# One decoder step on one core: the first six k tiles of the down projection as four pairs by seven products

## The chip, the cores and the metric

The kernel runs on one core of a Trainium2 chip. The metric is the device time of one launch in microseconds (us). TensorE (PE) multiplies into PSUM; VectorE (DVE), ScalarE (ACT) and GpSimd (POOL) do the rest; SyncE (SP) and POOL issue the transfers between DRAM and SBUF that this text speaks of. Each engine works through its own queue in order.

## The reference

One layer of a decoder, for 512 prompt tokens and 8 x 8 sample tokens, all in float32. The part that matters here is the feed-forward block behind the second norm:

```python
a, val = jnp.split(h2 @ w_up, 2, axis=-1)                # 1024 -> 2 x 2816
ac, new_ffn = _causal_conv(a, ffn_buf, ffn_conv_w)       # width 3, along the tokens
x = x + g2 * ((jax.nn.gelu(ac, approximate=False) * val) @ w_down)   # 2816 -> 1024
```

## The kernel before

Activations lie transposed: 128 features by 576 token columns (512 prompt, 64 sample) are one tile. w_up gives 22 "up tiles" m = 0 to 21; each has a gate and a value half, a convolution of three taps, a gelu and a product, t. The 22 tiles t are the k tiles of the down projection, which has 8 output tiles, m = 0 to 7.

Float32 accuracy comes from splitting each operand into a high and a low part (`split`: ACT writes the high part, DVE subtracts it for the low one) and from three passes of TensorE: high by high, high by low, low by high. A full product (`product`) of n k tiles is 6n matmuls: three passes by two column groups of 256 and 320.

Up tiles 4 to 21 and the down projection's last eight k tiles use `pair_product` instead: a two-by-two block product with seven products in place of eight (after Strassen and Winograd), each of 12 matmuls of 288 columns. It runs through seven parts into three PSUM banks X, Y and Z. Between parts it calls functions that the caller hands over as steps 0 to 7: step 0 before part 1, step n after part n. Part 5 writes bank Y, DVE reads it (`gate1`, rows pad), and part 7 writes Y again. X of an up tile is read by `times` one job later (rows cy).

The weights of a pair come from `pair_weights`: two raw blocks ra and rb of eight k tiles, and four sums of halves in place (sums1: s3 and rb; sums2: ra twice), each 128 x 512. Then A (ah, al), B (bh, bl), C (ch, cl) and D (dh, dl) are split: h is ACT's high part (whi, wh), l is DVE's low part (wlo, wl). Weights of job n + 1 are prepared beside job n by `beside_pair`, which says at which step; raw blocks of job n + 2 are loaded.

The order before: up tiles 0 to 3 as full products, up 4 to 7 as pairs, the down projection of k tiles 0 to 7 as eight full products, up 8 to 21 as pairs, the down projection of k tiles 8 to 13 as eight full products with other work beside them, and that of k tiles 14 to 21 as pairs. From the second norm on PE, ACT and DVE run in the order of the code (`pinned`); POOL's and SP's queues are ordered by a scheduler. Line 114 is the helper that issues for all engines in order, so instructions are told apart by tile names.

POOL does small things here: the copies of the convolution's state (sto, pad<-stF), the sample columns of `times` (cy<-p,y), and DMAs that add while they transfer.

Of the kernel before, what the change touches and what calls it, by code (L numbers as in the profile page):

```python
# [16 lines left out]
P = 128  # L17
# [57 lines left out]
def step_kernel(ctx: ExitStack, tc: tile.TileContext, ins: dict, outs: list):  # L75
# [15 lines left out]
    def nm(s):  # L91
        cnt[0] += 1
        return f"{s}{cnt[0]}"
# [31 lines left out]
    def pf(ps):  # L125
        return ps[:, 256:832]
# [303 lines left out]
            self.low(self.x1, self.r1)  # L430
            self.low(self.n4, self.r0[:, :HT])

    def pair_weights(ra, rb, moved="", narrow=True):

        c0, c1 = slice(0, 4), slice(4, 8)
        w = {}

        def add(out, x, y):
            dve.tensor_tensor(out=out, in0=x, in1=y, op=ALU.add)

        def tiles():
            return [wp.tile([P, NK, P], F32R, tag=t, name=nm(t), bufs=S_BUFS) for t in ("whi", "wlo")]
# [12 lines left out]

        def s3_slots():
            if not narrow:
                return [x[:, 0:4, :] for x in tiles()]
            return slot("wh", F32R, [P, 4, P]), slot("wl", F32R, [P, 4, P])

        def sums1():
            w["raw"] = slot("s3", shape=[P, 4, P])
            add(w["raw"], ra[:, c0], rb[:, c0])
            add(rb[:, c0], rb[:, c0], rb[:, c1])

        def sums2():
            add(ra[:, c0], ra[:, c0], rb[:, c0])
            add(ra[:, c1], ra[:, c1], ra[:, c0])

        def named(n0, n1, name):  # L470
            hi, lo = w[name]
            w[n0] = (lambda k: hi[:, k, :]), (lambda k: lo[:, k, :])
            if n1:
                w[n1] = (lambda k: hi[:, k + 4, :]), (lambda k: lo[:, k + 4, :])
# [15 lines left out]
    def pair_product(w, x, steps, out_a0, out_a1, out_b0, out_b1, apart=False):  # L490

        X, Y = (halves(mmps())[1][:, :HT] if apart or n else aux()[:, :HT] for n in range(2))
        Z = aux()[:, :HT]
        p5 = slot("p5")[:, :HT]

        def part(bank, wn, xn_, more=True):

            (hi, lo), xs = w[wn], x[xn_]  # L500
            for k in range(4):
                xh, xl = xs[k]
                passes = (hi(k), xh), (hi(k), xl), (lo(k), xh)
                for n, (wt, xx) in enumerate(passes):
                    matmul(
                        bank, wt, xx, start=not more and k + n == 0, stop=k + n == 5,
                        skip_group_check=more,
                    )
# [1322 lines left out]
    class FfnTile:  # L1831
# [37 lines left out]
            self.t = conv_times(ps, self.y)  # L1869

        def high(self):
            if self.m >= FB:
                fc.append(self.t)
                return
            self.hi = slot("fh", F32R)
            act.activation(self.hi, self.t, AF.Copy)

        def low(self):
            if self.m >= FB:
                return  # L1880
            lo = slot("fl", F32R)
            dve.tensor_tensor(out=lo, in0=self.t, in1=self.hi.bitcast(F32), op=ALU.subtract)
            fa.append((self.hi, lo))

    class FfnPair(FfnTile):
# [6 lines left out]
        def prepare(self):  # L1892
            self.w, self.steps = pair_weights(*self.raws)
            return self.steps

        def run(self, steps):
# [22 lines left out]
        def times(self):  # L1919
# [5 lines left out]
                out=b8(sv(t)), in0=b8(self.x1[:, n:]), in1=b10(self.y)[:, :, 0:8], op=ALU.mult  # L1925
            )

    def merged(*parts):

        out = {}  # L1930
# [6 lines left out]
    def beside_pair(p, t):  # L1937
# [14 lines left out]

    def down_load(m, m0, m1):
# [27 lines left out]
    for dst, w in zip(first, ws):  # L1981
        for g, k in pend[-2:]:
            kstep(dst, w, h2, k, (g,))
    made2, made3, fa, fc = {}, {}, [], []

    tiles = [FfnTile(m) for m in range(4)]
    ops = [PairOperands(h2, kp, made2, h2_raw) for kp in range(4)]
# [71 lines left out]
    steps["dl"]()  # L2059

    n3 = [op.n3 for op in ops]
    pairs = {4: pair, 5: nxt}
    for m0, m1 in FCH:
        if m0:
            fa = []
        before = None
        for m in range(max(m0, 4), m1):
            pair = pairs.pop(m)
            beside = []
            if m == 4:  # L2070
                beside = [{
                    1: n3, 2: [tiles[3].gelu], 5: [lambda: tiles[3].times(v3)],
                    6: [tiles[3].high, tiles[3].low],
                }]
            if m + 1 < m1:
                if m + 2 < m1:
                    pairs[m + 2] = FfnPair(m + 2)
                beside.append(beside_pair(before, pairs[m + 1].prepare()))
            else:
                wd = {}  # L2080
                raw = [down_load(j, m0, min(m1, FB)) for j in range(4 if m1 > FB else 2)]
                beside.append(beside_pair(before, None))
                beside.append({2: [lambda: wd.update({0: split_w(raw[0])})],
                               5: [lambda: wd.update({1: split_w(raw[1])})]})
            pair.run(merged(*beside))
            before = pair
        if m1 == NF:
            break
        before.first_tap()
        before.taps()  # L2090
        before.gelu()
        before.times()
        before.high()
        before.low()
        if m1 < NF:
            pairs = {m1: FfnPair(m1)}
            steps = None
            ps = [mmps() for _ in range(2)]
            n = m1 - m0
            for k0, k1 in ((0, n - 2), (n - 2, n)):  # L2100
                for j in range(2):
                    for k in range(k0, k1):
                        kstep(halves(ps[j]), wd[j], fa, k)
            wd[2] = split_w(down_load(2, m0, m1))
            for j in range(2):
                residual(pf(ps[j]), x1[j], 40 + j)
            for m in range(2, NK):
                if m + 1 < NK:
                    wd[m + 1] = split_w(down_load(m + 1, m0, m1))
                acc_m = product(wd[m], fa)  # L2110
                if m == 4:
                    steps = in_turn(pairs[m1].prepare())
                    steps[0]()
                elif m > 4:
                    steps[m - 3]()
                if m == NK - 1:
                    pairs[m1 + 1] = FfnPair(m1 + 1)
                residual(acc_m, x1[m], 40 + m)
    acc3 = slot("acc")
    r3 = cp.tile([P, 8], F32, tag="r3", name="r3")  # L2120

# [37 lines left out]
        ops[kp].sums()  # L2159

    def next_down():
        wd[len(wd)] = split_w_moved(wd_raw.pop(len(wd)))

    def next_raw():
        j = len(wd) + len(wd_raw)
        wd_raw[j] = down_load(j, m0, FB)

    def finish():
        before.times()
# [117 lines left out]
```

## Time and profile before

| | us |
|---|---|
| median of three runs | 960.41 (959.83 to 961.05) |
| span of the profiled execution | 958.8 |
| busy: PE / DVE / ACT / POOL in the span | 944.6 / 725.8 / 549.1 / 132.9 |
| up tiles 4 to 7 as pairs end, old down stage begins | 653.4 |
| the old down stage ends, up tile 8 begins | 706.0 |
| the last down products begin, about | 857 |

The profile gives the span of its execution, from the first to the last instruction, and no separate launch time; the three runs lie 1.0 to 2.2 us above the span. Rows of the order of time read: start, length, engine, line, operation, out<-in, shape, count, and in brackets idle time before it and who ended it.

### The profile page before, as it was taken

The numbers are of one execution on the slowest core, as the hardware profiler recorded it, in microseconds if no ns is written. First come the engines' busy times: TensorE is split into PE (matmuls) and PEld (weight loads), VectorE is DVE, ScalarE is ACT, GpSimd is POOL, SyncE is SP. The second block draws the span as 40 slices with busy tenths as digits, with TensorE's granted clock in tenths as the row PEclk, the third lists the DMA queues.
The fourth block names the chain that finished last, engine by engine and source line by source line (L and its number), as shares of the span: only waits on it lengthen the run. The fifth ranks groups of instructions, "written<-read, shape, count | busy, mean of one in ns | idle before, by whom it ended". The sixth has DMA issues, their size and how long they took to land.

```text
span 958.8 us, 18738 instructions
## 1 busy us (share of the span) xinstructions
PE 944.6 (99%) x7290; PEld 909.4 (95%) x7290; DVE 725.8 (76%) x1355; ACT 549.1 (57%) x1058; POOL 132.9 (14%) x317
## 2 busy tenths in 40 slices
PE   7999999999999999999999999999999999999997
PEld 5799999999999899999889999999999999999997
DVE  4788988875876867876677588995559998968864
ACT  5474768745665447865344566653226565546664
POOL 2123121101201012210001130100000011101110
PEclk9999999999999999999999999999999999999999
DMA  9984233426546768799985732232323233228542
GB/s 275 332 249 110 77 93 100 150 71 172 122 128 201 237 220 215 198 247 285 302 282 113 185 86 66 85 106 67 110 89 90 88 90 109 84 82 173 128 96 99
DMA packets 182651, 144.09 MB, mean 150 GB/s; under 512 B 7688, under 2 KB 162124, under 8 KB 182274
## 3 DMA queue, kind: packets, MB, share of 16 engines
q1 hardware_dynamic: 172546, 111.72, 38.9%
q0 software_dynamic: 9872, 30.92, 14.1%
q8 instruction: 57, 0.93, 0.4%
q14 instruction: 32, 0.26, 0.1%
q10 hardware_dynamic: 144, 0.26, 0.1%
HBM read 113.89 MB, written 12.07 MB: 131 GB/s over the span
## 4 chain that ended last, share of the span: by engine, by line
PE 90%; DMA 3%; ACT 2%; issue 2%; DVE 1%; SPq 1%; POOL 0%; POOLq 0%; ACTq 0%; DVEq 0%
PE mm L114 50%; PE aux L114 37%; PE aux L1281 2%; PE aux L1185 2%; DMA ad<-in_w_ada 1%; SPq L538 1%; DMA wlo<-raw 1%; DMA raw<-in_w_down 1%; ACT whi L114 1%; DMA x<-in_x_prompt 1%; ACT wlo L114 0%; ACT xh L114 0%; ACT sg L114 0%; ACT nh L114 0%; DVE tl L114 0%
## 5 line engine op out<-in xcount | busy, mean ns | idle before, releaser
L114 ACT ACTIVATE whi<-raw 128x1024 fp32r<-128x1024 f32 (+3 forms) x186 | 188.8, 1023 | 81.7 <-DVE raw L114 28.4
L114 DVE TENSOR_TENSOR wlo<-raw,whi 128x1024 fp32r<-128x1024 f32 (+2 forms) x163 | 192.3, 1185 | 37.0 <-ACT whi L114 36.2
L114 PE MATMUL aux<-2l,whi 128*128 128x288 f32 (+2 forms) x232 | 68.4, 295 | 0.0
L114 PE MATMUL aux<-2h,whi 128*128 128x288 f32 (+2 forms) x232 | 68.3, 295 | 0.0
L114 PE MATMUL aux<-2h,wlo 128*128 128x288 f32 (+2 forms) x232 | 68.3, 295 | 0.0
L114 DVE TENSOR_TENSOR raw<-raw 128x512 f32<-128x512 f32 x88 | 61.6, 700 | 2.8
L114 PE MATMUL mm<-hh,whi 128*128 128x256 f32 (+2 forms) x264 | 60.6, 303 | 0.5 <-ACT hh L114 0.5
L114 PE MATMUL mm<-hh,wlo 128*128 128x256 f32 (+2 forms) x264 | 58.3, 295 | 0.0
L114 PE MATMUL aux<-hh,whi 128*128 128x288 f32 (+1 forms) x196 | 57.5, 300 | 0.0
L114 PE MATMUL mm<-hl,whi 128*128 128x256 f32 (+2 forms) x264 | 57.4, 295 | 0.1
L114 PE MATMUL aux<-hl,whi 128*128 128x288 f32 (+1 forms) x196 | 56.5, 295 | 0.0
L114 PE MATMUL aux<-hh,wlo 128*128 128x288 f32 (+1 forms) x196 | 56.4, 295 | 0.0
L114 PE MATMUL mm<-fh,whi 128*128 128x256 f32 x224 | 48.0, 296 | 0.4 <-DVE rt L114 0.4
L114 PE MATMUL mm<-fh,wlo 128*128 128x256 f32 x224 | 47.9, 295 | 0.0
L114 PE MATMUL mm<-fl,whi 128*128 128x256 f32 x224 | 47.8, 295 | 0.0
L114 PEld LDWEIGHTS mm<-hh,whi 128*128 128x128 f32 x264 | 43.8, 188 | 1.5 <-ACT hh L114 1.1
L114 PEld LDWEIGHTS mm<-hl,whi 128*128 128x128 f32 x264 | 44.0, 188 | 0.7 <-DVE hl L114 0.5
L114 PEld LDWEIGHTS mm<-hh,wlo 128*128 128x128 f32 x264 | 44.6, 188 | 0.0
L114 PEld LDWEIGHTS aux<-2h,whi 128*128 128x128 f32 x232 | 43.7, 188 | 0.0
L114 PEld LDWEIGHTS aux<-2h,wlo 128*128 128x128 f32 x232 | 43.7, 188 | 0.0
L114 PEld LDWEIGHTS aux<-2l,whi 128*128 128x128 f32 x232 | 43.6, 188 | 0.0
L114 DVE SCALAR_TENSOR_TENSOR y<-pad,par2T,y 128x592 f32<-128x592 f32 x44 | 36.6, 833 | 9.0 <-ACT y L114 8.2
(409 smaller groups left out, 3104.9 us busy)
## 6 DMA issues: line engine op xcount, KB each, us to landing
raw<-in_w_in SPq DMA_DIRECT2D x52, 512.0 KB, 4.7
raw<-in_w_up SPq DMA_DIRECT2D x44, 512.0 KB, 3.9
ada<-in_w_ada SPq DMA_DIRECT2D x64, 256.0 KB, 5.4
wlo<-raw POOLq DMA_DIRECT2D x17, 512.0 KB, 4.8
ad<-in_w_ada SPq DMA_DIRECT2D x32, 256.0 KB, 6.2
raw<-in_w_down SPq DMA_DIRECT2D x16, 512.0 KB, 4.0
sg_dram<-sg POOLq DMA_DIRECT2D x16, 288.0 KB, 4.4
gt<-sg_dram SPq DMA_DIRECT2D x16, 288.0 KB, 5.7
```

Source lines behind the costliest of these rows:

```text
L114: done = getattr(self.engine, name)(*args, **kwargs)
L538: return tc.keep_in_program_order(nc.sync.dma_start(dst, src))
L1185: done = nc.tensor.matmul(O[HALF[par], c], vt(i - nkt + 1 + kt)[:, hd * 64 : hd * 64 + 64], pts[kt][:, par * 256 : par * 256 + 256], start ...
L1281: done = nc.tensor.matmul(ps[32 * j : 32 * j + 32, :], cT[:, k, :], cols[k][j], start=(k == 1), stop=(k == NK - 2),)
```

## The change

The order becomes: up 4 to 8, then the down projection of k tiles 0 to 5 as four pair jobs (`DownPair`, output tiles 0 and 1, 2 and 3, 4 and 5, 6 and 7; half is 3 k tiles, so a part is 9 matmuls), then up 9 to 21, then eight full products over k tiles 6 to 13. The t of tiles 0 to 5 are kept raw (`fr`) and made into pair operands by `RawOperands` beside up 5 to 8. Tiles 6, 7 and 8 are written to DRAM by POOL (`away`), read back by SP beside up 21 and split there. The last products take the k tiles in the order 9 to 13, 6, 7, 8 (`turned`).

The four sums of each pair prepared from up 5 on go to POOL (`prepare(pool)`). In `beside_pair`, bh moves from step 1 to 3, bl from 2 to 4, ch from 5 to 6, cl from 5 to 7, and sums2 from 3 to 0.

```diff
-FCH = [(0, 8), (8, 22)]
-FB = 14
+FA, FB = 6, 14
+AWAY = 3
+DOWN_AT = 9
...
-    def pair_weights(ra, rb, moved="", narrow=True):
+    def pair_weights(ra, rb, moved="", narrow=True, adder=None):
...
+        nk = ra.shape[1]
+        half = nk // 2
...
-            dve.tensor_tensor(out=out, in0=x, in1=y, op=ALU.add)
+            (adder or dve).tensor_tensor(out=out, in0=x, in1=y, op=ALU.add)
...
         def high(self):
-            if self.m >= FB:
+            if self.m < FA:
+                fr.append(self.t)
+            elif self.m < FA + AWAY:
+                pool.dma_start(away[self.m - FA], self.t)
+            elif self.m >= FB:
                 fc.append(self.t)
...
+    class DownPair:
+        def __init__(self, m):
+            self.m = m
+            self.raws = [down_load(m + e, 0, FA) for e in range(2)]
+        def prepare(self, adder=None):
+            self.w, t = pair_weights(*self.raws, adder=adder)
+            return t
+        def run(self, steps):
+            pair_product(self.w, made_d["op"], steps, *mix_outs(self.m, 40))
...
-            0: [f("ah"), g("first_tap"), f("sums1"), f("al"), g("taps")],
-            1: [f("bh")],
-            2: [f("bl")],
-            3: [g("gelu"), f("dh"), f("sums2")],
-            4: [f("dl")],
-            5: [f("ch"), g("times"), f("cl")],
-            6: [g("high")],
-            7: [g("low")],
+            0: [f("ah"), g("first_tap"), f("sums1"), f("al"), g("taps"), f("sums2")],
+            3: [g("gelu"), f("bh"), f("dh")],
+            4: [f("bl"), f("dl")],
+            5: [g("times")],
+            6: [f("ch"), g("high")],
+            7: [f("cl"), g("low")],
...
+    def fetch():
+        for j in range(AWAY):
+            t = slot("cy")
+            nc.sync.dma_start(t, away[j])
+            back.append(t)
...
+    order = [("up", m) for m in range(4, DOWN_AT)]
+    order += [("down", m) for m in range(0, NK, 2)]
+    order += [("up", m) for m in range(DOWN_AT, NF)]
...
+        ("up", 5): {1: [raw_op(0, "sums")], 2: [raw_op(0, "first", "first_low")],
+                    5: [raw_op(0, "second")], 6: [raw_op(0, "second_low")]},
...
+        ("up", 8): {1: [raw_op(0, "third")], 2: [raw_op(0, "third_low"), raw_op(1, "third")],
+                    4: [raw_op(1, "third_low")], 5: [raw_op(2, "third")], 6: [raw_op(2, "third_low")]},
...
+            beside.append(beside_pair(before, stages[n + 1].prepare(pool)))
```

Up 6 and 7 have the rows of up 5 for operand pairs 1 and 2. On PE the program goes from 6830 to 6794 rows; up to up 4 it is the same but for the line numbers.

POOL beside up 12, which prepares the weights of up 13, before (raw are the weight blocks, s the third sum):

```order
L1229 MEMSET pad_9374 128x2
L1850 COPY pad_9374<-stF 128x8x2
L1924 TENSOR_TENSOR cy_9473<-p_9241,y_9383 128x64
L1258 COPY sto<-pad_9374 128x2
L1259 COPY sto<-pad_9374 128x16
```

and in the changed kernel:

```order
L1232 MEMSET pad_9363 128x2
L1853 COPY pad_9363<-stF 128x8x2
L115 TENSOR_TENSOR s_9374<-raw_9221,raw_9223 128x512
L115 TENSOR_TENSOR raw_9223<-raw_9223 128x512
L115 TENSOR_TENSOR raw_9221<-raw_9221,raw_9223 128x512
L115 TENSOR_TENSOR raw_9221<-raw_9221 128x512
L1931 TENSOR_TENSOR cy_9459<-p_9230,y_9372 128x64
```

The four sums now stand between the state's copy and the tile's sample columns.

DVE at the same place, before, from the first sum to the pad rows (y are the taps):

```order
L114 TENSOR_TENSOR s_9385<-raw_9232,raw_9234 128x512
L114 TENSOR_TENSOR raw_9234<-raw_9234 128x512
L114 TENSOR_TENSOR wlo_9381<-raw_9232,whi_9380 128x1024
L114 SCALAR_TENSOR_TENSOR y_9383<-pad_9236,par2T,y_9383 128x592 x2
L114 TENSOR_TENSOR wlo_9405<-raw_9234,whi_9404 128x1024
L114 TENSOR_TENSOR raw_9232<-raw_9232,raw_9234 128x512
L114 TENSOR_TENSOR raw_9232<-raw_9232 128x512
L114 TENSOR_TENSOR wl_9436<-s_9385,wh_9435 128x512
L114 TENSOR_TENSOR pad_9374<-mm_9377,p_9379 128x224
```

and in the changed kernel:

```order
L115 TENSOR_TENSOR wlo_9370<-raw_9221,whi_9369 128x1024
L115 SCALAR_TENSOR_TENSOR y_9372<-pad_9225,par2T,y_9372 128x592 x2
L115 TENSOR_TENSOR wlo_9423<-raw_9223,whi_9422 128x1024
L115 TENSOR_TENSOR wl_9426<-s_9374,wh_9425 128x512
L115 TENSOR_TENSOR pad_9363<-mm_9366,p_9368 128x224
```

The four sums have left DVE's queue; the second wlo still stands ahead of pad.

ACT at the same place, before (y<-pad is the first tap, y<-y the gelu, mm<-aux and aux<-mm are the bank copies behind parts 1 and 3):

```order
L114 ACTIVATE y_9383<-pad_9236,par2T 128x592
L114 ACTIVATE mm_9377<-aux_9376 128x288
L114 ACTIVATE whi_9404<-raw_9234 128x1024
L114 COPY p_9379<-aux_9378 128x288
L114 ACTIVATE aux_9378<-mm_9377 128x288
L114 ACTIVATE y_9383<-y_9383 128x592
L114 ACTIVATE wh_9435<-s_9385 128x512
```

and in the changed kernel:

```order
L115 ACTIVATE y_9372<-pad_9225,par2T 128x592
L115 ACTIVATE mm_9366<-aux_9365 128x288
L115 COPY p_9368<-aux_9367 128x288
L115 ACTIVATE aux_9367<-mm_9366 128x288
L115 ACTIVATE y_9372<-y_9372 128x592
L115 ACTIVATE whi_9422<-raw_9223 128x1024
L115 ACTIVATE wh_9425<-s_9374 128x512
```

The second high part, whi, has moved from ahead of the gelu to behind it.

More of the change, by code (lines that the diff above doesn't have):

```diff
@@ L457, in s3_slots @@
             if not narrow:
-                return [x[:, 0:4, :] for x in tiles()]
-            return slot("wh", F32R, [P, 4, P]), slot("wl", F32R, [P, 4, P])
+                return [x[:, c0, :] for x in tiles()]
+            return slot("wh", F32R, [P, half, P]), slot("wl", F32R, [P, half, P])
         def sums1():
-            w["raw"] = slot("s3", shape=[P, 4, P])
+            w["raw"] = slot("s3", shape=[P, half, P])
             add(w["raw"], ra[:, c0], rb[:, c0])
@@ L500, in part @@
             (hi, lo), xs = w[wn], x[xn_]
-            for k in range(4):
+            for k in range(len(xs)):
                 xh, xl = xs[k]
@@ L505, in part @@
                     matmul(
-                        bank, wt, xx, start=not more and k + n == 0, stop=k + n == 5,
+                        bank, wt, xx, start=not more and k + n == 0, stop=(k, n) == (len(xs) - 1, 2),
                         skip_group_check=more,
@@ L1983, in step_kernel @@
             kstep(dst, w, h2, k, (g,))
-    made2, made3, fa, fc = {}, {}, [], []
+    made2, made3, made_d, fa, fc, fr = {}, {}, {}, [], [], []
+    away = dp.tile([AWAY, P, NT], F32, name="away")
     tiles = [FfnTile(m) for m in range(4)]
@@ L2061, in step_kernel @@
     n3 = [op.n3 for op in ops]
[L2062 to L2118, printed above, removed]
@@ new lines, in step_kernel, with raw_op, f, split_back @@
+    ops_d = {}
+    def raw_op(kp, *names):
+        def f():
+            if kp not in ops_d:
+                ops_d[kp] = RawOperands(fr[kp], fr[kp + FA // 2], made_d)
+            for name in names:
+                getattr(ops_d[kp], name)()
+        return f
+    back = []
+    def fetch():
[3 more added lines that the diff above has]
+            back.append(t)
+    def split_back():
+        fa.extend([split_slot(t, "f") for t in back])
@@ new lines, in step_kernel @@
+    before = None
+    for n, at in enumerate(order):
+        job = stages.pop(n)
+        beside = []
+        if n == 0:
+            beside.append({
+                1: n3, 2: [tiles[3].gelu], 5: [lambda: tiles[3].times(v3)],
+                6: [tiles[3].high, tiles[3].low],
+            })
+        beside.append(first_ops.get(at, {}))
+        if n + 2 < len(order):
+            kind, m = order[n + 2]
+            stages[n + 2] = FfnPair(m) if kind == "up" else DownPair(m)
+        if n + 1 < len(order):
+            beside.append(beside_pair(before, stages[n + 1].prepare(pool)))
+        else:
+            raw = [down_load(j, FA, FB) for j in range(4)]
+            beside.append(beside_pair(before, None))
+            beside.append({2: [lambda: wd.update({0: turned(split_w(raw[0]))})], 3: [fetch],
+                           5: [lambda: wd.update({1: turned(split_w(raw[1]))})], 6: [split_back]})
+        job.run(merged(*beside))
+        before = job if at[0] == "up" else None
```

32 lines of the change are left out of this document (21 added, 11 removed).

## The prediction

> **What bounds the kernel now.** I read the page's first two parts, then the chain of waits, then the busy time by stage, then the order of time on each engine inside one up tile.
>
> ```profile
> span 958.8 us, 18738 instructions
> PE 944.6 (99%) x7290; PEld 909.4 (95%) x7290; DVE 725.8 (76%) x1355; ACT 549.1 (57%) x1058; POOL 132.9 (14%) x317
> PE   7999999999999999999999999999999999999997
> PEclk9999999999999999999999999999999999999999
> ```
>
> TensorE is filled from end to end at full clock, so only fewer matmuls, or a new wait of TensorE, can move the end. POOL is nearly empty. The sum below is made against this execution's span, 958.8 us. The three runs (median 960.4) lie 1.0 to 2.2 us above that, so I add differences to 960.4.
>
> The chain of waits, start and length in us:
>
> ```profile
> 653.36 52.65 PE mm L114 x396
> 717.13 3.19 PE aux L114 x24
> 720.32 1.58 PE mm L114 x12
> 728.24 3.19 PE aux L114 x24
> ```
>
> The first row is the old down projection of k tiles 0 to 7: 52.65 / 396 = 0.1330 us for each matmul. Up tiles repeat every 728.24 - 717.13 = 11.11 us, seven parts of twelve matmuls at 1.58 to 1.59 us, or 0.132 us for each matmul. (The mean of one in the page's groups counts overlap twice; this spacing is the price.)
>
> ```profile
> core 0: us, PE busy (x) PEld busy (x) DVE busy (x) ACT busy (x) POOL busy (x), PEclk, DMA share, GB/s
> 653.36:706.02 52.66, 52.66 (x399) 52.66 (x398) 26.31 (x43) 13.80 (x16) 0.83 (x5) 1.00 0.31 91
> 728.24:739.34 11.10, 11.10 (x87) 11.10 (x86) 10.44 (x17) 6.87 (x11) 0.83 (x5) 1.00 0.33 97
> ```
>
> In an up tile DVE is busy 10.44 of 11.10 us, yet TensorE never waits. In the old down stage DVE is half idle. The change turns that stage into pairs and gives DVE the operands of those pairs as well.
>
> **The matmuls.** Removed: 8 x 8 x 6 + 8 x 6 x 6 = 672. New: 4 pairs x 7 products x 9 = 252, and 8 x 8 x 6 = 384. Time: 672 x 0.133 = 89.4 us against 252 x 0.132 + 384 x 0.133 = 84.4. That is **-5.0 us**, certain as long as TensorE doesn't wait.
>
> **The adds on POOL.** 21 pairs (17 up, 4 down) have four adds each: 68 of 512 elements and 16 of 384. DVE loses about 0.69 us for each and POOL takes them. The trace has no wide two-operand add on POOL. The nearest rows are five adds of 64 elements and three copies of 64 in a row:
>
> ```profile
> 550.08 1.31 POOL L1740 TENSOR_TENSOR t<-x,A 128x64 f32<-128x64 f32 x5
> 299.53 0.59 POOL L1571 COPY ot<-od 128x64 f32<-128x64 f32 x3 [0.75 <-issue]
> ```
>
> One add is 0.26 us, one copy 0.20. Upper bound for 512 elements: all of it scales, 8 x 0.26 = 2.1 us. Lower bound: DVE's own time for the size, 0.69 us. If the second operand's 0.06 us for 64 elements is the price of each operand, an element costs 1.9 ns and 512 cost 0.26 + 448 x 1.9 ns = **1.1 us** (384: 0.85). I take that, since it is the only value that uses both rows. The Trainium skill (GPSIMD Engine Reference, 3.1 Elementwise) gives 2.6 cycles an element at 1.2 GHz; its estimate for 512 is also 1.1 us, and no run here shows it yet. By throughput POOL then has room: 4 x 1.1 + 0.83 = 5.2 of 11.1 us.
>
> But POOL and DVE hold each other up. Two engines, one place, between the same us:
>
> ```profile
> 844.63 0.68 DVE L114 TENSOR_TENSOR raw<-raw,raw 128x512 f32<-128x512 f32 x1
> 845.35 0.82 DVE L114 TENSOR_TENSOR raw<-raw 128x512 f32<-128x512 f32 x1
> 845.31 0.32 POOL L1924 TENSOR_TENSOR cy<-p,y 128x64 f32<-128x64 f32 x1 [8.34 <-ACT y L114]
> 845.61 0.64 POOL L1850 COPY pad<-stF 128x16 f32<-128x16 f32 x1
> L1850 POOL COPY pad<-stF x12: 207/427/642, 725.9 to 845.6; 128x16 f32<-128x16 f32 x12
> ```
>
> The DVE add that starts 0.04 us behind a POOL add takes 0.82 instead of 0.68 us. The POOL copy that comes behind this DVE add ends 0.08 us after it and takes 0.64 us, where the fastest of the twelve takes 0.207. So an instruction of one engine stands still while the other's runs. With 64 elements that costs 0.1 us; with 512 it would cost up to 1.1 us each time. The Trainium skill (SBUF — State Buffer, Who interferes with whom) says so: a DVE instruction with two SBUF inputs and a GpSimd instruction that reads SBUF exclude each other for the whole instruction, whichever comes second. These rows agree at small size.
>
> **One up tile, laid end to end.** DVE's order of time:
>
> ```profile
> 729.74 1.22 DVE L114 TENSOR_TENSOR wlo<-raw,whi 128x1024 fp32r<-128x1024 f32 x1
> 730.88 1.70 DVE L114 SCALAR_TENSOR_TENSOR y<-pad,par2T,y 128x592 f32<-128x592 f32 x2
> 732.49 1.22 DVE L114 TENSOR_TENSOR wlo<-raw,whi 128x1024 fp32r<-128x1024 f32 x1
> 734.97 0.68 DVE L114 TENSOR_TENSOR wl<-s,wh 128x512 fp32r<-128x512 f32 x1
> 736.20 0.52 DVE L114 TENSOR_TENSOR pad<-mm,p 128x224 f32<-128x224 f32 x2 [0.56 <-PE mm L114]
> 736.64 0.45 DVE L114 TENSOR_TENSOR cy<-aux,y 128x288 f32<-128x288 f32 x1
> 737.01 0.42 DVE L114 TENSOR_TENSOR cy<-p,y 128x224 f32<-128x224 f32 x1
> 738.48 0.45 DVE L114 TENSOR_TENSOR p<-aux,p 128x288 f32<-128x288 f32 x1
> 738.85 0.74 DVE L114 TENSOR_TENSOR fl<-cy,fh 128x576 fp32r<-128x576 f32 x1
> ```
>
> Distances from row to row: low half of a weight (wlo) 1.14, taps 1.61, pad 0.44, cy 0.37 and 0.34, p 0.37, fl 0.66, wl 0.66. On ACT:
>
> ```profile
> 733.10 0.40 ACT L114 ACTIVATE aux<-mm 128x288 f32<-128x288 f32 x1 [1.22 <-PE mm L114]
> 733.41 0.69 ACT L114 ACTIVATE y<-y 128x592 f32<-128x592 f32 x1
> 735.14 1.06 ACT L114 ACTIVATE whi<-raw 128x1024 fp32r<-128x1024 f32 x1 [0.52 <-DVE raw L114]
> ```
>
> After the change the high half of the second weight (whi) comes behind the gelu (y<-y), which waits for DVE's taps; DVE then waits 1.7 us for gelu and whi before its next wlo. Before, whi came ahead of gelu. The new round from pad to pad: 0.44 + 0.37 + 0.34 + 0.37 + 1.14 + 1.14 + 1.61 + 1.7 + 1.14 + 0.66 = 8.9 us, without fl. It fits 11.1 as long as the adds are free. With exclusion the fourth add falls into the 1.7 us wait and 0.4 us of the first lies beside p, which reads PSUM; the other 0.7 + 1.1 + 1.1 = 2.9 us are inserted. **11.8 us: +0.7** for each of seven tiles, and with fl (five tiles) 12.5: +1.4. Sum 11.9 us for the twelve tiles that prepare up 10 to 21. What is late is pad: it must have read its bank before part 7 writes there. Part 5 to part 7 leaves 1.59 - 0.52 = 1.07 us, absorbed once; after that TensorE takes DVE's pace.
>
> **Up 5 to 7 with operands.** DVE and ACT get into the same round: a low half of 576 (0.66), two half-width subtractions (0.75, priced as p), ACT's high half of 576 (0.66, as y<-y) and the bank copy (0.37): 11.35 us. Now all four adds are inserted but for the 0.4: 15.3 us, **+4.2 each, 12.7 together**. Up 8 has the third operands of three pairs (3.1) and low halves of 768 (0.9 each) and 384 (0.5): 1.5 + 0.66 + 1.14 + 0.9 + 1.61 + 3.1 + 0.9 + 0.5 = 10.3, with adds 3.3, of which 1.2 beside PSUM reads: 12.4, +1.3.
>
> **Down pairs** need 7 x 9 x 0.132 = 8.3 us. Their residuals, from the groups of DVE's instructions (count, busy us, mean ns):
>
> ```profile
> L114 DVE SCALAR_TENSOR_TENSOR x<-mm,modT,x 128x288 f32<-128x288 f32 x5 | 2.6, 514 | 1.8 <-PE mm L114 1.8
> L114 DVE SCALAR_TENSOR_TENSOR x<-p,modT,x 128x224 f32<-128x224 f32 x10 | 4.5, 452 | 0.4
> L114 DVE TENSOR_TENSOR rt<-mm,modT 128x64 f32<-128x64 f32 x19 | 4.1, 215 | 0.0
> L114 DVE TENSOR_TENSOR x<-x,rt 128x64 f32<-128x64 f32 x32 | 7.3, 227 | 1.0
> ```
>
> Less 0.07 us of overlap each, 2 x 0.44 + 2 x (0.37 + 0.38 + 0.15 + 0.16) = 3.0 us. Low halves 3 x 0.9 + 0.5 = 3.2, adds 3.3, of which 1.6 beside PSUM reads: 7.9 us, fits. The first also has tile 8's taps and cy and the third pair's last operand (1.61 + 0.71 + 1.04 = 3.4): +3.0. The last prepares up 9 at full width (0.9 + 1.1 more): 9.9, +1.6.
>
> **Hidden.** Three tiles to DRAM and back are 288 KB each at a DMA share near 0.33; the last down products are given them as k tiles 5 to 7, needed 5 x 0.8 = 4 us after the first begins. If late, that costs one wait of some 2 us. The final products grow from 4.8 to 6.4 us each, which gives ACT, DVE and the DMA sums more cover. POOL's queue: the writes to DRAM stand ahead of a down pair's adds and wait for cy, but the adds are due only three parts later. SP's loads wait for cl, which moves behind p; they have a round to land.
>
> **Sum.** 11.9 + 12.7 + 1.3 + 3.0 + 1.6 - 1.1 = +29.4; with -5.0, +24.4: 984.8 us. The lower end of exclusion is where adds always meet a DVE that reads PSUM or sits idle: a steady tile then needs 7.2 (8.9 without the wait) + 4.4 - 1.2 = 10.4 us and fits; up 5 to 7 need 7.2 + 0.66 x 2 + 1.5 + 4.4 - 1.2 = 13.2 (+2.1 each), the rest as above: 6.3 + 5.9 - 1.1 - 5.0 = +6.1, 966.5 us. In-order engines don't arrange themselves so well; I take a value near the first, **980 us**.
>
> **Rivals.**
> - The other side: wide POOL adds slip between DVE's reads. For it: the losses seen are only 0.1 us, and no 512-wide add was ever seen. Against it: the two rows above. Then -5.0, less 0.25 x 3 in up 5 to 7 and 1.3 at the first down pair: about 957. It decides where an add costs DVE under 0.55 us, because (11.1 - 8.9) / 4 is what a round can take. Chance 0.24.
> - Exclusion, but well interleaved: about 966.5. For it: add one can start behind pad's copies, a round ahead of its need. Chance 0.22 (962.3 to 972).
> - POOL at the 2.1 us bound: DVE's round is 8.9 + 1.7 + 2.1 + 2.1 + 0.4 = 15.2 us, twelve tiles lose 49 us, over 1030. Against it: an add has a fixed part. Chance 0.05.
>
> **Numbers.** The forecast (972 to 998) has 0.43; near no change 0.06. Within 0.2% (1.9 us, about what a measurement can tell): 0.06; faster 0.24; slower 0.70. Range 956 to 998: at the top the add is 1.35 us (each 0.1 us costs about 5 us in all), the bottom takes in most of the faster case.
>
> **What shows it.** Right: POOL's 512-wide adds at 1.1 us or more, mean wlo on DVE well over 1.22 us, and TensorE idle behind DVE's pad in up 5 to 8 and 10 to 21, where the distance of tiles goes from 11.1 to 11.8 or more. Wrong: wlo still at 1.22 beside a running add, or tiles still 11.1 us apart.

## The result, and the profile after

The changed kernel takes 989.3 us (median of four runs, 988.79 to 990.28), the kernel before 960.73 us beside it (959.83 to 962.84). The ratio is 1.0297, with a 95% interval from 1.0283 to 1.0312: about 28.6 us slower. The forecast was 980 us with a range to 998. The profiled execution has a span of 987.0 us, 28.2 more than that of before.

The first rows of the page, with TensorE's row and its granted clock in 40 slices:

```profile
span 987.0 us, 18843 instructions
PE 946.9 (96%) x7254; PEld 907.0 (92%) x7254; DVE 751.9 (76%) x1329; ACT 561.7 (57%) x1084; POOL 259.8 (26%) x404
PE   6999999999999999999999999977889999999997
PEclk8999999999999999999999999999999999999999
```

TensorE has 36 matmuls fewer, as predicted, but for the first time it has slices at 7 and 8 tenths in the middle: up 6 to the last of the new down pairs. POOL's busy time has doubled. DVE has 26 instructions fewer and yet 26 us more of busy time.

Who TensorE waited for between 600 and 890 us (engine and tile waited for: us in all, times, longest):

```profile
PE mm L115 <- ACT aux L115: 10.0, 4, 3.2
PE mm L115 <- DVE pad L115: 8.2, 13, 1.3
PE mm L115 <- DVE p L115: 5.0, 3, 2.3
PE mm L115 <- DVE wlo L115: 2.7, 2, 1.7
```

Before, TensorE had no wait there (the same view of that stretch is empty). The job lengths, from the starts of the first matmuls, give the account (all at 11.10 and 8.35 would be 211.0 us):

| stage | full speed | after | loss |
|---|---|---|---|
| up 5, 6, 7, 8 | 4 x 11.10 | 13.93, 16.09, 14.39, 15.61 | 15.6 |
| down pairs | 4 x 8.35 | 10.53, 11.44, 8.54, 12.13 | 9.2 |
| up 9, 10 | 2 x 11.10 | 11.11, 11.09 | 0 |
| up 11 to 15 | 5 x 11.10 | 12.33 to 12.37 | 6.2 |
| up 16 to 20 | 5 x 11.10 | 11.61 to 11.64 | 2.6 |

The losses are 33.6 us; less the 5.0 us of removed matmuls that makes 28.6, beside 28.2 measured between the spans.

What lengthened is seen on DVE and POOL in one of the later up tiles. DVE, order of time:

```profile
750.92 2.61 DVE L115 SCALAR_TENSOR_TENSOR y<-pad,par2T,y 128x592 f32<-128x592 f32 x2
755.24 1.23 DVE L115 TENSOR_TENSOR wlo<-raw,whi 128x1024 fp32r<-128x1024 f32 x1 [1.71 <-ACT whi L115]
...
758.12 0.44 DVE L115 TENSOR_TENSOR p<-aux,p 128x288 f32<-128x288 f32 x1
758.49 1.95 DVE L115 TENSOR_TENSOR wlo<-raw,whi 128x1024 fp32r<-128x1024 f32 x1
760.36 1.85 DVE L115 TENSOR_TENSOR fl<-cy,fh 128x576 fp32r<-128x576 f32 x1
```

POOL in the same stretch:

```profile
751.14 1.75 POOL L115 TENSOR_TENSOR raw<-raw,raw 128x512 f32<-128x512 f32 x1 [1.90 <-DVE wlo L115]
...
757.91 1.45 POOL L115 TENSOR_TENSOR s<-raw,raw 128x512 f32<-128x512 f32 x1
759.44 2.16 POOL L115 TENSOR_TENSOR raw<-raw 128x512 f32<-128x512 f32 x1
```

The low half that begins while POOL's s is running takes 1.95 us instead of 1.23. POOL's next add, whose row begins at 759.44, stands still until that low half is done and ends at 761.60; fl waits in turn: 1.85 us instead of 0.74. The two taps take 2.61 instead of 1.70. But p<-aux,p, which has one operand in PSUM and lies wholly beside the same s, takes 0.44 us, as it did before (0.45).

The groups of DVE's instructions from 735 to 860 us (count, busy us, mean ns):

```profile
L115 DVE TENSOR_TENSOR wlo<-raw,whi 128x1024 fp32r<-128x1024 f32 x32 | 46.3, 1460 | 18.1 <-ACT whi L115 18.1
L115 DVE SCALAR_TENSOR_TENSOR y<-pad,par2T,y 128x592 f32<-128x592 f32 x22 | 28.3, 1284 | 0.4
L115 DVE TENSOR_TENSOR fl<-cy,fh 128x576 fp32r<-128x576 f32 x5 | 9.2, 1847 | 0.0
L115 DVE TENSOR_TENSOR p<-aux,p 128x288 f32<-128x288 f32 x10 | 4.4, 444 | 0.0
```

The forecast's mechanism is there. How much of the loss it makes, and what the rest is, the experiments tell.

### The profile page after: what moved, and what is told of

Same layout as the page of the kernel before. It is cut to its first block, busy times and chain, and to the rows that moved or that the text cites. A ratio compares the mean times of both kernels' runs of the same rounds, so it can differ in the third digit from the quotient of the medians.

```text
span 987.0 us, 18843 instructions
## 1 busy us (share of the span) xinstructions
PE 946.9 (96%) x7254; PEld 907.0 (92%) x7254; DVE 751.9 (76%) x1329; ACT 561.7 (57%) x1084; POOL 259.8 (26%) x404
## 4 chain that ended last, share of the span: by engine, by line
PE 77%; DVE 13%; ACT 5%; issue 3%; DMA 1%; SPq 0%; POOL 0%; ACTq 0%; DVEq 0%
PE mm L115 44%; PE aux L115 30%; DVE wlo L115 5%; DVE y L115 2%; ACT whi L115 2%; PE aux L1284 2%; PE aux L1188 1%; DVE wl L115 1%; DVE fl L115 1%; DMA x<-in_x_prompt 1%; DVE pad L115 1%; DVE cy L115 1%; DVE p L115 0%; DMA q<-low 0%; DVE tw L115 0%
## 5 line engine op out<-in xcount | busy, mean ns | idle before, releaser
L115 DVE TENSOR_TENSOR wlo<-raw,whi 128x1024 fp32r<-128x1024 f32 (+3 forms) x167 | 207.5, 1253 | 58.8 <-ACT whi L115 58.3
L115 ACT ACTIVATE whi<-raw 128x1024 fp32r<-128x1024 f32 (+3 forms) x190 | 191.8, 1017 | 43.2 <-DVE raw L115 12.0
L115 POOL TENSOR_TENSOR raw<-raw 128x512 f32<-128x512 f32 (+1 forms) x42 | 67.5, 1607 | 3.1
L115 DVE SCALAR_TENSOR_TENSOR y<-pad,par2T,y 128x592 f32<-128x592 f32 x44 | 53.4, 1214 | 4.7 <-ACT y L115 3.9
L115 POOL DMA_DIRECT2D wlo<-raw x23 | 20.0, 870 | 134.9 <-ACT wlo L115 60.6
L115 PE MATMUL mm<-nh,whi 128*128 128x288 f32 x120 | 37.4, 311 | 13.2 <-DVE pad L115 8.2
L115 POOL TENSOR_TENSOR raw<-raw,raw 128x512 f32<-128x512 f32 (+1 forms) x21 | 33.3, 1586 | 49.3 <-DVE wlo L115 45.6
L115 ACT ACTIVATE aux<-mm 128x288 f32<-128x288 f32 x48 | 18.9, 395 | 45.4 <-PE mm L115 45.0
L115 ACT ACTIVATE mm<-aux 128x288 f32<-128x288 f32 x45 | 17.9, 398 | 46.4 <-PE aux L115 46.4
```

Source lines behind the costliest of these rows:

```text
L115: done = getattr(self.engine, name)(*args, **kwargs)
```

## The experiments

**1. The same change with the four sums left on DVE.** The theory: POOL's sums hold DVE, so without them most of the loss goes. The rival: the new stage and the moved steps lose it anyway.

```diff
-            beside.append(beside_pair(before, stages[n + 1].prepare(pool)))
+            beside.append(beside_pair(before, stages[n + 1].prepare()))
```

> The changed kernel with one thing undone: the four sums of every pair run on DVE again. Theory (POOL's wide adds and DVE's two-operand instructions stand still for each other): an up tile's DVE round becomes 8.9 us plus 1.3 us of sums (the other two fall into the wait for gelu and whi), 10.2 to 10.9 us, so up 9 to 21 go back to 11.1 us each; up 5 to 7 need about 12.7 us (+1.5 each), up 8 and the first down pair lose 1 and 3 us. About 960 to 966 us, and DVE's second taps row and fl go back to 0.83 and 0.75 us. Rival (the new order of the steps and the operands of the down pairs cost the time, the place of the sums does not): stays above 980 us.

Measured: 970.0 us (969.32 to 970.73) against 960.47; ratio 1.0095 (1.0078 to 1.0112). Up 9 to 20 are back at 11.1 us each. Of the 28.6 us, 19.3 are gone with the one argument. The rival, over 980, falls; but the expectation (960 to 966) was 4 us too low. Up 5 to 8 still take 13.24, 14.93, 13.85 and 14.28 us. Its waits of TensorE from 600 to 890 us:

```profile
PE mm L115 <- ACT aux L115: 6.3, 4, 2.0
PE mm L115 <- DVE p L115: 2.4, 3, 1.3
PE mm L115 <- DVE pad L115: 2.2, 3, 1.3
```

So something other than POOL makes up 5 to 8 slow; experiments 4 and 5 look for it.

**2. POOL equally busy, but without reading.** Each sum on POOL is left out, and three memsets of its output stand in its place, so the weights aren't the right ones. The theory: POOL's reading of SBUF holds DVE, not its queue, its dependences or its writing.

```diff
-            (adder or dve).tensor_tensor(out=out, in0=x, in1=y, op=ALU.add)
+            if adder is None:
+                dve.tensor_tensor(out=out, in0=x, in1=y, op=ALU.add)
+            else:
+                for _ in range(3):
+                    nc.gpsimd.memset(out, 1.0)
```

> The changed kernel with each of POOL's sums left out and three memsets of the same output tile in its place, so that POOL is still busy for about as long and the waits for POOL stay, but it reads nothing from SBUF. Theory (what excludes is the reading on both sides): DVE's rows go back to their own lengths (fl 0.75, wlo 1.22, a tap 0.83 us), up 9 to 21 take 11.1 us, 956 to 962 us in all. Rival 1 (POOL's queue is late, whatever it does): 980 us or more. Rival 2 (any POOL instruction on SBUF excludes DVE, writes too): the rows stay long and the time stays near 980 to 990 us.

Measured: 960.67 us (959.99 to 962.01); ratio 1.0002 (0.9992 to 1.0011). POOL's busy time is 251 us in the span, nearly that of the changed kernel. POOL's group from 600 to 880 us, and DVE's fl from 735 to 860 us (shortest, median and longest ns), first in the changed kernel and then here:

```profile
L446 POOL MEMSET raw<- 128x512 f32 x153 | 74.1, 526 | 66.0 <-DVE wlo L115 47.0 <-DMA raw<-in_w_up 11.1 <-DVE cy L115 7.9
```

```profile
L115 DVE TENSOR_TENSOR fl<-cy,fh x5: 1842/1847/1852, 748.0 to 797.4; 128x576 fp32r<-128x576 f32 x5
```

```profile
L115 DVE TENSOR_TENSOR fl<-cy,fh x9: 745/747/759, 738.7 to 854.3; 128x576 fp32r<-128x576 f32 x9
```

From 735 to 860 us DVE's low halves (1.22 us), taps (0.83) and fl are as long as before; only wl is 0.07 us longer in the mean, and POOL's small reading rows are still there. The whole 28.6 us between this kernel and the changed one is the price of the sums, with the same order, steps and queues. (A memset waits for the tile that it overwrites, not for the operand that it no longer reads, so the waits on POOL's side are not quite the same.) It also says that the change without any sums at all is no faster than before: up 5 to 8 lose 4.3 us and the down pairs 1.7, which eats the 5.0 us of matmuls. (The two losses less the matmuls make +1.0 us, the medians differ by 0.2; where the other 0.8 lies isn't followed here.)

**3. Only the sums moved, in the kernel before.** The theory: the exclusion costs by itself, without the new stage.

```diff
...
-                beside.append(beside_pair(before, pairs[m + 1].prepare()))
+                beside.append(beside_pair(before, pairs[m + 1].prepare(pool)))
```

> The kernel before with only this changed: the sums of the weights that are prepared beside a pair (up 6, 7 and 10 to 21, with up 5 and 9) run on POOL; steps, down projection and order stay. Theory (exclusion): each of these tiles has 4 adds of 1.3 us against DVE, and whi of the second weight now waits for them early on ACT, ahead of bank copies; 1 to 2 us for each of some 15 tiles, 975 to 990 us. Rival (POOL takes the sums for nothing, the down pairs cost the time): 960 us, within 2.

Measured: 968.5 us (967.63 to 969.29); ratio 1.0082 (1.0067 to 1.0097). The direction is right and the size was expected too large: tiles go from 11.10 to 11.77 (those with fl) and 11.42 (those without), not to 12 or 13. One such tile:

```profile
core 0: us, PE busy (x) PEld busy (x) DVE busy (x) ACT busy (x) POOL busy (x), PEclk, DMA share, GB/s
766.00:777.80 11.80, 11.41 (x86) 11.17 (x85) 11.77 (x13) 6.92 (x12) 8.83 (x10) 1.00 0.30 88
```

DVE had 10.44 of 11.10 us busy with its own sums; it now has 13 instructions instead of 17 and 11.77 of 11.80 us busy. Taking work off DVE has filled it up, since an instruction that stands still counts as busy. The same sums cost 12.35 and 11.63 us a tile with the changed kernel's steps, so the moved steps add 0.58 and 0.2 us to a tile here; experiment 9 has the new order with the old steps and sums on POOL, and its later tiles are those of this run.

**4. Experiment 1 with the step table of before.** The theory: the operands of the pairs fill DVE in up 5 to 8, whatever the steps. The rival: the moved steps cost 3 us or more.

```diff
-            0: [f("ah"), g("first_tap"), f("sums1"), f("al"), g("taps"), f("sums2")],
-            3: [g("gelu"), f("bh"), f("dh")],
-            4: [f("bl"), f("dl")],
-            5: [g("times")],
-            6: [f("ch"), g("high")],
-            7: [f("cl"), g("low")],
+            0: [f("ah"), g("first_tap"), f("sums1"), f("al"), g("taps")],
+            1: [f("bh")],
+            2: [f("bl")],
+            3: [g("gelu"), f("dh"), f("sums2")],
+            4: [f("dl")],
+            5: [f("ch"), g("times"), f("cl")],
+            6: [g("high")],
+            7: [g("low")],
```

> The first of these (sums on DVE) with the old order of the steps of a pair's preparation too, so that of the change only the down pairs, their operands and the way by DRAM stay. Theory: up 9 to 21 as before, 11.1 us; up 5 to 8 and the first down pair are full on DVE (10.0 + 2.6 us own work beside 11.1) and lose 1 to 2 us each: 960 to 966 us, within 2 of the first one. Rival (the moved steps are a cost of their own): 3 us or more faster than the first one.

Measured: 966.86 us (966.39 to 967.63); ratio 1.0066 (1.0051 to 1.0081). That is 3.1 us less than experiment 1, just over the rival's bar of 3 and not within the 2 us of the theory: the moved steps do cost. (In the profiled executions up 5 to 8 differ by 4.3 us, and some 1.5 of that is a drop of TensorE's clock that only experiment 1's profile has, see the last section; whether its other launches had the drop isn't shown.) Up 5 to 8 take 12.69, 13.47, 13.53 and 12.34 us; the down pairs are the same to 0.1 us. What is left above the kernel before, with sums on DVE and the old steps, is 7.6 us in up 5 to 8 and 3.8 in the down pairs, less the 5.0 of the matmuls.

**5. The operands spread over five tiles.** From experiment 4: one more up tile stands before the down pairs, and each tile gets about one operand, mostly at late steps, behind the bank copies.

```diff
-AWAY = 3
-DOWN_AT = 9
+AWAY = 4
+DOWN_AT = 10
...
-        ("up", 5): {1: [raw_op(0, "sums")], 2: [raw_op(0, "first", "first_low")],
-                    5: [raw_op(0, "second")], 6: [raw_op(0, "second_low")]},
...
+        ("up", 5): {1: [raw_op(0, "sums")], 5: [raw_op(0, "first")], 6: [raw_op(0, "first_low")]},
+        ("up", 6): {1: [raw_op(1, "sums")], 5: [raw_op(0, "second")], 6: [raw_op(0, "second_low")]},
+        ("up", 7): {1: [raw_op(2, "sums")], 5: [raw_op(1, "first")], 6: [raw_op(1, "first_low")]},
...
```

> Sums on DVE with the old order of steps, and the down pairs one up tile later: they stand behind up 9, four tiles go by way of DRAM, and the operands of the three pairs are made beside up 5 to 9, ACT's part of each behind its bank copies. Theory (DVE is what is full in that stretch): an up tile's own DVE work there is 9.8 + 2.3 = 12.1 us beside 11.1, so each of five tiles loses 1 us (before: 1.2 to 2.4 us each of four), the down pairs lose 4 us as before: 962 to 965 us. Rival (the loss there is ACT's high parts standing ahead of the bank copies, not DVE's load): the five tiles take 11.1 to 11.4 us each and the whole 959 us or less.

Measured: 962.25 us (960.83 to 963.72, eleven runs) against 961.21; ratio 1.0017 (1.0008 to 1.0026), in the expected range. Up 5 to 9 lose 2.9 us instead of 7.6 in four tiles, less than the 1 us each that was expected; the down pairs lose 4.8.

**6. Experiment 5, and DVE relieved by DMA.** For the jobs from up 5 to the last down pair, the low halves of B and D are made by ACT and a DMA that adds (`moved`, which the program has for other stages), so DVE has two subtractions fewer in each.

```diff
+MOVED = {n: "BD" for n in range(2, 11)}
...
-            beside.append(beside_pair(before, stages[n + 1].prepare()))
+            beside.append(beside_pair(before, stages[n + 1].prepare(moved=MOVED[n + 1] if n + 1 in MOVED else "")))
```

> The kernel with spread operands, and in the jobs from up 5 to the last down pair the low halves of B and D are made by ACT and an adding DMA in place of DVE (1.1 and 0.6 us of DVE in a job of up tiles, 1.4 in a down pair). Theory: DVE then has 10.3 us beside 11.1 in an up tile and about 7 beside 8.3 in a down pair; both fit, so the five fewer us of matmuls are kept: 955 to 958 us, faster than before by 0.3 to 0.5%. Rival (ACT, with 10 to 11 us then, becomes the bound, or the adding DMA's 5 us is late): 960 to 966 us.

Measured: 959.02 us (median of eleven; ten of them 957.79 to 959.97, and one launch of 2345.76 us that nothing here explains); ratio 0.9976 (0.9967 to 0.9985). It is faster than before, by less than expected. Up 5 to 9 are all 11.09 to 11.12; the down pairs keep 9.56, 9.56, 8.76 and 9.47. The order of time in the second of them, on ACT:

```profile
690.76 0.85 ACT L116 ACTIVATE whi<-raw 128x768 fp32r<-128x768 f32 x1 [1.86 <-DVE raw L116]
692.54 0.40 ACT L116 ACTIVATE aux<-mm 128x288 f32<-128x288 f32 x1
```

ACT waits 1.86 us for a sum of DVE, and the bank copy (aux<-mm) that TensorE needs stands behind it: a part of 9 matmuls leaves 1.2 us where one of 12 leaves 1.6. Experiment 8 takes this up.

**7. Copies in place of the sums.** Each sum on POOL is left out again, and two copies that read one operand stand in its place. The theory: any POOL instruction that reads SBUF holds DVE. The rival: it takes two operands.

```diff
-            (adder or dve).tensor_tensor(out=out, in0=x, in1=y, op=ALU.add)
+            if adder is None:
+                dve.tensor_tensor(out=out, in0=x, in1=y, op=ALU.add)
+            else:
+                for _ in range(2):
+                    nc.gpsimd.tensor_copy(out=out, in_=y)
```

> The changed kernel with each of POOL's sums left out and two copies with one operand of the same size in its place: POOL reads SBUF, but only one operand at a time. Theory (any POOL instruction that reads SBUF excludes DVE's second operand for its whole length): with copies of 0.4 to 0.5 us, DVE's taps and fl rows stay lengthened (taps pair over 2.0, fl over 0.9 us) and the time lies at 970 to 985 us, above the 960.7 of the memsets. Rival (only two-operand instructions of POOL exclude): the rows are back at 1.7 and 0.75 us and the time is 960 to 962 us.

Measured: 981.7 us (981.27 to 984.72); ratio 1.0225 (1.0208 to 1.0241). POOL's group of copies, and DVE's fl from 735 to 860 us:

```profile
L446 POOL COPY raw<-raw 128x512 f32<-128x512 f32 x102 | 93.8, 921 | 18.7 <-issue 13.4 <-DVE wlo L115 1.8
```

```profile
L115 DVE TENSOR_TENSOR fl<-cy,fh x5: 1159/1160/1161, 744.0 to 793.9; 128x576 fp32r<-128x576 f32 x5
```

POOL is about as busy as with memsets (264 and 251 us in the span), and 21 us more are lost: one operand read is enough. Whether the second operand or the length of one instruction makes the other 7.6 us to the changed kernel isn't tried. Fl takes 1.16 us behind a copy, 1.85 behind a sum and 0.75 beside a memset.

**8. Experiment 6 with a step table of the down pairs' own.** Beside a down pair B's high and low parts and the last up tile's taps come one step later than in the old table, so that the bank copies stand ahead of the high part that waits for sums.

```diff
+        if in_down:
+            return {
+                0: [f("ah"), f("sums1"), f("al")],
+                1: [g("first_tap"), g("taps")],
+                2: [f("bh")],
+                3: [f("bl"), g("gelu"), f("dh"), f("sums2")],
+                4: [f("dl")],
+                5: [f("ch"), g("times"), f("cl")],
...
```

> The kernel with spread operands and low halves by DMA, and in the jobs of the down pairs B's high half on ACT comes one step later, behind the bank copies of parts 1 and 2, and the first tap of the last up tile one step later. Theory: what still holds the down pairs (9.56, 9.56, 8.76 and 9.47 us where 63 matmuls take 8.35) is ACT's bank copy standing behind a high half that waits for DVE's sums; about 0.9 us go from three of the four: 956 to 957.5 us, 0.3 to 0.5% faster than before. Rival (DVE's load in the down pairs holds them): no change, 958.5 to 959.5 us.

Measured: 956.64 us (955.61 to 957.14) against 960.63; ratio 0.9952 (0.9939 to 0.9966). This version beats both kernels, by 4.0 and about 33 us. Its two stages by window, up 5 to 9 and the down pairs:

```profile
621.80:677.30 55.50, 55.50 (x422) 55.50 (x421) 49.02 (x86) 43.19 (x71) 15.97 (x36) 1.00 0.68 154
677.30:712.00 34.70, 34.31 (x255) 33.61 (x254) 32.34 (x68) 24.36 (x41) 8.66 (x14) 1.00 0.79 183
```

TensorE has no gap in the up tiles and 0.4 us in the down pairs, which take 34.6 us, 1.2 above full speed (9.10, 8.83, 8.35 and 8.35). Up 10 behind them takes 11.78, 0.7 more than full speed, with a wait of 0.4 us for an adding DMA.

**9. Experiment 6 with the sums on POOL again.** The theory: with operands spread and DVE relieved, POOL's sums still hold DVE. The rival: DVE now has the room.

```diff
-... stages[n + 1].prepare(moved=MOVED[n + 1] if n + 1 in MOVED else "")))
+... stages[n + 1].prepare(pool, moved=MOVED[n + 1] if n + 1 in MOVED else "")))
```

> The kernel with spread operands and low halves by DMA, and all sums from up 5 on on POOL again. It asks if POOL's sums pay where DVE has room for them. Theory (each sum of 1.3 us on POOL holds DVE for up to 1.15 us, and takes only 0.62 us from it): no; up 11 to 20 as in the kernel before with POOL's sums (11.8 and 11.4 us), up 5 to 9 11.1 to 12 us: 963 to 972 us. Rival (the loss came only where DVE was over full): within 2 us of the kernel with spread operands and low halves by DMA, 957 to 961 us.

Measured: 970.19 us (968.99 to 971.42); ratio 1.0097 (1.0083 to 1.0111), 11.2 us above experiment 6 on the same steps and operands. Up 6 to 8 take 11.50 to 11.78, up 9 15.71, and up 12 to 20 what they took in experiment 3: 11.75 to 11.79 with fl, 11.4 without. The rival falls. (In the profiled execution some 1.5 us of up 9's loss are again the clock of the last section.)

## Why the prediction was right, and where its sum was not

**What is shown.** The sums on POOL cost 28.6 us against the same queue with memsets (experiment 2), 19.3 us against sums on DVE (experiment 1), and 8.0 and 11.2 us in two other surroundings (experiments 3 and 9), each time in tiles where DVE's instructions with two SBUF operands are long (fl 1.85, and 1.49 in the two others, for 0.75). Reading is what does it (experiments 2 and 7). So the forecast's main reason, taken from two rows with a 64-element add and a small copy, held at 512 elements. The Trainium skill (SBUF — State Buffer, Who interferes with whom) says that a DVE instruction with two SBUF inputs contends with a GpSimd instruction that reads SBUF, not with one that only writes it, and that a DVE instruction with at most one SBUF input (outside modes that use both ports) doesn't contend. The traces agree where it was tried: fl takes 0.75 us beside memsets and 1.16 beside copies, and p, with one operand in PSUM, 0.444 us in the mean beside sums.

**The matmuls.** 36 fewer, worth 5.0 us: the count is in the page, and the account above closes with that value to 0.4 us.

**The add on POOL.** Taken at 1.1 us (512) and 0.85 (384). An add that starts 0.04 us ahead of a DVE instruction with two SBUF operands, and that instruction, read so:

```profile
830.40 1.28 POOL L115 TENSOR_TENSOR s<-raw,raw 128x512 f32<-128x512 f32 x1
```

```profile
830.44 1.49 DVE L115 TENSOR_TENSOR cy<-p,y 128x224 f32<-128x224 f32 x1
```

All sums that read both ra and rb and write one of them (shortest, median and longest ns):

```profile
L115 POOL TENSOR_TENSOR raw<-raw,raw x21: 1010/1749/1759, 613.2 to 858.7; 128x512 f32<-128x512 f32 x17, 128x384 f32<-128x384 f32 x4
```

The shortest of all 512-wide sums take 1.28 us, the shortest of 384, 1.01. The estimate of 1.1 us, and the same figure from the Trainium skill (GPSIMD Engine Reference, 3.1 Elementwise), lay 14% low. The median of 1.75 holds the waiting for DVE. But the row of DVE behind the add is only 1.07 us longer than before (0.42), so an add's whole length isn't what it costs.

**The steady up tiles.** Predicted 12.5 us with fl and 11.8 without; measured 12.35 and 11.63. In the chain of waits DVE's low halves lie 12.35 us apart, and parts of TensorE in the tiles without fl 11.63:

```profile
749.86 1.14 DVE wlo L115
762.21 1.14 DVE wlo L115
818.59 1.86 PE mm L115 x12
830.22 1.86 PE mm L115 x12
```

Pad is what TensorE waits for there, as predicted (6.0 us in ten waits from 735 to 868 us). The round itself came out as laid, but partly by luck. Three rows of DVE stand behind adds and are longer than before: without fl cy<-p,y by 1.07 us, a low half by 0.72 and the taps by 0.90, which is 2.7 us where 2.9 were inserted, and 8.9 + 2.7 = 11.6; with fl it is a low half, fl (1.10) and the taps, again 2.7. With the measured 1.28 us for an add, the prediction's own way of inserting gives 0.9 + 1.28 + 1.28 = 3.4: the add was priced too low, and what DVE feels of one (0.7 to 1.1 us) too high. The slack absorbed two whole tiles, up 9 and 10, not 1.1 us: 8.8 us lost instead of 10.8.

**Up 5 to 8.** Predicted 12.7 + 1.3 = 14.0, measured 11.1 + 4.5 = 15.6: the sum is near by luck. Up 5 to 7 lost less than predicted, although 1.5 us of their 11.1 is the clock of the last section, which no term had; up 8 lost three times as much as predicted. And the step "what is late is pad" failed here. Of the waits from 622 to 682 us only 2.2 us are for pad; 10.0 are for ACT's bank copy (the first line of the waits above). On ACT the cause stands one row ahead of the copy:

```profile
629.39 0.68 ACT L115 ACTIVATE xh<-cy 128x576 fp32r<-128x576 f32 x1 [3.56 <-DVE cy L115]
629.98 0.39 ACT L115 ACTIVATE aux<-mm 128x288 f32<-128x288 f32 x1
...
644.64 0.68 ACT L115 ACTIVATE xh<-cy 128x576 fp32r<-128x576 f32 x1 [4.88 <-DVE cy L115]
```

The operand's high part xh waits 3.56 and 4.88 us for DVE's operand sums (cy), which come behind two low halves and the taps; the bank copy, which DVE never touches, waits in ACT's queue behind xh. The prediction laid out DVE's round and did not say who stands behind the waiting instruction on ACT. This wait isn't POOL's alone: in up 5 to 8 it has 6.3 us with the sums on DVE (experiment 1), 1.5 with the old steps as well (experiment 4), and none with the operands behind the copy too (experiment 5).

**The down pairs.** This was the term with the largest error: 4.6 us predicted (3.0 + 0 + 0 + 1.6), 9.2 measured (2.2 + 3.1 + 0.2 + 3.8). DVE's busy time was laid against 8.3 us of matmuls and found to fit, but nothing was said of deadlines inside the job. TensorE waited there for DVE's p, which must have read bank Y before part 7 (5.0 us in three waits), and for C's low half (2.7 us in two). Without POOL's reading the four pairs lose 1.7 us (experiment 2), so the shortfall is the exclusion's, in a job whose parts are 1.2 us long.

**The sum.** Predicted 10.8 + 14.0 + 4.6 - 5.0 = 24.4 us, measured 8.8 + 15.6 + 9.2 - 5.0 = 28.6.

**The rivals.** "Well interleaved" (966.5) and "adds slip between" (957) are both refuted by the rows; POOL at 2.1 us an add by its 1.28. The second rival was also mis-sized: adds that cost nothing give 960.7 us (experiment 2), because the operands in up 5 to 8 cost 4.3 us where 0.25 x 3 was allowed, and the pairs 1.7 for 1.3. With the steps as they stand, then, the change isn't faster even with sums that hold nobody.

**The value.** The working gave 984.8 us, and 980 was taken as a step toward the better case. That step went the wrong way: the sum itself was already 4.5 us low.

## What to carry to other kernels

Before moving work from VectorE to GpSimd, look at where its operands lie: while GpSimd reads SBUF, VectorE's instructions with two SBUF operands stand still, so here four sums of 0.69 us taken off VectorE cost it more than they gave, in the three surroundings that were tried. ScalarE and an adding DMA could take other work off VectorE, two low halves a job, and that made the kernel 3.2 us shorter (experiment 6 against 5). And when work is put beside a filled TensorE, don't ask only whether an engine's busy time fits: list each thing that TensorE needs by a certain part (a bank read, a bank copy, a low half), and look at what stands ahead of it in the same queue and what that waits for. Changes of order, with the sums on VectorE, were worth 3.1, 4.6 and 2.4 us here (experiments 4, 5 and 8; 5 also sends one more tile through DRAM), together about twice what the removed matmuls are worth.

## What the runs showed of the hardware beyond that

**A long wait of TensorE costs a second time.** In up 6 it was idle for 3.19 us. The matmuls behind that gap, start and length:

```profile
645.68 0.40 PE L115 MATMUL mm<-2h,wh 128*128 128x288 f32 x1 [3.19 <-ACT aux L115]
...
646.83 0.45 PE L115 MATMUL mm<-2l,wh 128*128 128x288 f32 x1
647.07 0.45 PE L115 MATMUL mm<-2h,wl 128*128 128x288 f32 x1
...
650.10 0.29 PE L115 MATMUL aux<-2h,whi 128*128 128x288 f32 x1
```

For about 3.4 us they stand 0.24 us apart instead of 0.13, which loses some 1.5 us, and the granted clock of that stretch is 0.50. The length of the gap alone doesn't decide it. In experiment 1 a gap of 2.01 us in up 6 was followed by the same drop, while the gap of 2.32 us in up 7 of the changed kernel was followed by none.

What decides can be read from the traces. The clock's records in the traces change at steps of 3.413 us that the gaps don't shift: in the changed kernel the clock came to full at 21.91 us and fell at 646.55, 183 steps later, 0.87 us after work had resumed; in experiments 1 and 9 the same distance is 185 and 195 steps. So lay the 3.41 us steps over the trace and ask how long TensorE was busy in each. Steps of the changed kernel, with the columns of experiment 3 (behind the window its length and TensorE's busy time; the last but two is the granted clock):

```profile
643.14:646.55 3.41, 0.87 (x6) 0.87 (x7) 2.89 (x5) 1.91 (x4) 0.82 (x2) 1.00 0.00 0
646.55:649.97 3.42, 3.42 (x17) 3.42 (x16) 2.81 (x7) 2.68 (x4) 0.79 (x6) 0.50 0.07 18
656.79:660.21 3.42, 1.81 (x14) 1.58 (x12) 3.32 (x4) 0.32 (x1) 2.11 (x2) 1.00 0.05 15
721.65:725.06 3.41, 1.65 (x12) 1.65 (x13) 3.34 (x6) 0.62 (x1) 2.65 (x3) 1.00 0.52 154
```

and of experiment 1:

```profile
641.37:644.78 3.41, 1.40 (x11) 1.17 (x10) 2.88 (x6) 1.98 (x4) 0.31 (x1) 1.00 0.00 0
644.78:648.20 3.42, 3.42 (x16) 3.42 (x16) 2.83 (x6) 2.60 (x4) 0.68 (x5) 0.50 0.09 28
```

Once the clock was full, and up to the end of the kernel, the eleven traces have three drops. Ahead of them TensorE was busy for 0.87, 1.40 and (experiment 9) 0.62 us of a step. The least busy steps that no drop followed have 1.65 us and more. The gap of 2.32 us in up 7 fell across two steps and left 1.81 us in the emptier one. So a step in which TensorE idles for some 60% was followed here by one at half clock, and one in which it idles for half was not; where between 1.40 and 1.65 us the limit lies isn't shown.

The Trainium skill (TensorE: Matmul & The Clock Gate, Part 1) has the clock halve after at least one idle window of about 3.4 us and return after as much work, with windows that run freely. The free windows and the return agree; but no step ahead of a drop was wholly idle here, so the measurement decides: a gap of 2.0 us can be enough.

**Two limits of the exclusion.** Writing alone doesn't hold DVE: 252 memsets (up to 0.53 us each) left its long rows at the lengths of before. And it has nothing to do with how hard POOL works: memsets and copies kept POOL busy for 251 and 264 us, and 21 us lie between them.
